# Neighbourhood attention on 192 keys per half block, with three shared transposes per head and products in parts of 128 and 64 keys

## The chip, the cores and the metric

The kernel runs on one core of a Trainium2 chip. The metric is the device time of one execution in microseconds (us), and the number that counts is the median of several. A core has a matmul engine (TensorE, PE in the profile; its weight loads are PEld), a vector engine (VectorE, DVE), an activation engine (ScalarE, ACT), GpSimd (POOL) and SyncE (SP). Here SP issues all the DMAs. Matmuls write into PSUM, which has eight banks of 2 KB in each of its 128 partitions.

## What is computed

A trunk of two layers is applied to two requests of 512 tokens (s = 0 and s = 1), with 1024 channels and 16 heads of 64. Layer 0 is a bidirectional RWKV-7 scan. Layer 1, which is changed here, is attention on a grid of 8 rows by 64 columns: each token attends to all 8 rows and to a window of 16 columns about its own.

```python
GRID_W, WIN_ROWS, WIN_COLS = 64, 8, 16
Q_COL_BLOCK = 16
KEY_COL_SPAN = Q_COL_BLOCK + WIN_COLS          # 32 columns of keys for 16 columns of queries
...
s = jnp.einsum('bnqhd,bsnkhd->bhnqsk', qr, kr)
s = jnp.where(mask, s + bias, NEG_INF)
p = jax.nn.softmax(s.reshape(s.shape[:4] + (-1,)), axis=-1).reshape(s.shape)
return jnp.einsum('bhnqsk,bsnkhd->bnqhd', p, vr)
...
return (o.reshape(bsz, t, D_INNER) * jax.nn.silu(z)) @ w_o + b_o
```

## The kernel before

**Stages.** A prelude projects the first inputs, then a scan phase runs the eight recurrences with projections woven in between. Its instructions stand in an order that a planner in the kernel writes out. Then `rest` (L1724) begins, the part that matters here. There the frame's own scheduler sets the order on every engine: it takes the instructions as the generators emit them, by priority and by a timeline of its own. `rest` makes the remaining in-projections of request 0, the layer-0 output of request 1 (`out0`), the norm after it (`norm0`), the attention output of request 0 (`out1`), the in-projections and the attention of request 1, and `last` (L1502), the output of request 1.

**Matmuls of the projections.** Weights and activations are split into a high and a low part (`halves`, L373: ACT casts the high part, DVE subtracts for the low one). `gemm` (L420) makes a tile of 128x512 outputs with 24 matmuls, L426, L427 and L428 for each of eight slices; they write the tiles `pg` (two banks) or `pm`. L1538 to L1540 are the same for `last`.

**Attention.** `heads(s, p)` (L1394) is a generator that takes one pair of heads. `attention` (L1733) steps it between the slices of the projections, so that its short matmuls stand between the long ones. Tokens are in column order, so that 128 queries are 16 columns: a block n, of which there are four. A pair goes through the blocks in two half steps, `ns` = (0, 1) and (2, 3). There are 16 pairs (8 of each request), so 32 half steps. In each half step stand:

- **scores** (L1421): eight matmuls of 64 queries by 256 keys, on 64x64 tiles of TensorE, one for each block, half block a and head h. They write `sc`, one tile of two banks;
- **softmax**: for each block and head a row of DVE and ACT operations on 256 keys (L1430 adds the bias and takes the maximum, L1432, L1433 is the exponential on ACT, L1434, L1435);
- **transposes** (L1437): two of 128 keys for each block and head, eight in all, into `pt`; ACT copies them to `pts` (L1440);
- **products with v** (L1452): eight matmuls on 128x64 tiles, two key parts of 128 for each block and head, into `po`, one bank that serves the pair through both half steps.

After the second half step L1462 multiplies `po` by the gate z (`tmp` or `oa` takes the result), and for request 1 the result is split at once. Scores and products have a raised priority (`SHP`), and `behind` keeps the products of a half step together.

**Around it.** The bias of a pair comes in two DMAs of 384 KB into one buffer (`NBI` = 1). z is loaded behind the scores of the second half step. q, k, v and z go through DRAM. In `rest` the banks are `pg` 2, `pt` 2, `po` 1, `pm` 1, `sc` 2. `out1` takes `pm` and `pg` in turn, and `last` takes `pg`, `pm`, `pg`, `pt`. Between the two requests stands the norm: `rstds` (L447) sums squares with four matmuls (L452), takes the root on ACT (L455), forms a diagonal on DVE (L460) and spreads it with four matmuls (L464); then L1294 scales eight tiles on DVE, and L1295 adds the residual to them.

Of the kernel before, what the change touches and what calls it, by code (L numbers as in the profile page):

```python
# [10 lines left out]
F32 = mybir.dt.float32  # L11
F32R = mybir.dt.float32r
AF = mybir.ActivationFunctionType
ALU = mybir.AluOpType
# [4 lines left out]
P = 128  # L19
T = 512  # L20
D = 1024
KT = D // P
NP = 8
# [183 lines left out]
        return max([self.t["P"]] + list(self.tiles.values()))  # L207


class Thread:  # L210


# [22 lines left out]
class Trunk:  # L235
# [1 line left out]
    POST0, POST, POST2, POST3, NPA = 0.7, 1.0, 0.15, 0.66, 5  # L237
    HP, HS = (1000, 0), 1000
    SHP = 2000
    OUT1 = ("pm", "pg", "pm", "pg")  # L240
    LOW = 15
    LA = -40
    LATER = (0, 40, 0, 0)
    POST4 = 0.2
    LAST = ("pg", "pm", "pg", "pt")
    PG, PT, NK, NPT = 2, 2, 2, 3
    AHEAD, AHEADW, SCAN_A, SCAN_W = 0, 0, 300, 300
    NAB, NX, NR, NY, NSB, NBI = 2, 2, 2, 2, 4, 1
# [1145 lines left out]
    def heads(self, s, p):  # L1394

        nc = self.nc
        vt, act, gps = nc.vector, nc.scalar, nc.gpsimd
        b = lambda tag, shape=(P, T), n=1, dt=F32: self.t(tag, shape, n, dt, self.ap)
        bias = b("bias", (P, 2, 3, 256), self.NBI)
        for h in range(2):  # L1400
            self.load(bias[:, h].rearrange("p a b -> p (a b)"), self.a["rpb"][2 * p + h])
        q, k, v = (self.load(b(kind, n=2), self.sp[kind, s, p]) for kind in ("q1", "k1", "v1"))
        yield
        vtok = b("vtok", (P, 7, P), self.NK)
        for j0, j1 in ((0, 4), (4, 7)):
            ps = self.p("pt", (P, 4, P))
            for j in range(j0, j1):
                nc.tensor.transpose(ps[:, j - j0], v[:, 64 * j:64 * j + P], self.ident)
            act.copy(vtok[:, j0:j1], ps[:, 0:j1 - j0])
            yield  # L1410
        op = self.p("po", (P, 4, P))
        cols = (0, 8, 24, 32)
        for ns in ((0, 1), (2, 3)):

            sc = self.p("sc", (P, 2, 2, 256))
            with self.tc.high_priority(self.SHP):
                for n in ns:
                    for a in (0, 64):
                        for h in range(2):
                            hs = slice(64 * h, 64 * h + 64)  # L1420
                            nc.tensor.matmul(  # L1421
                                sc[a:a + 64, h, n % 2], q[hs, n * P + a:n * P + a + 64], k[hs, 8 * cols[n]:8 * cols[n] + 256],
                                start=True, stop=True)
            pts = []
            for n in ns:
                pt = self.p("pt", (P, 2, 2, P))
                for h in range(2):
                    sb = b("sb", (P, 256), self.NSB)
                    mx = b("mx", (P, 4), 6)
                    vt.tensor_tensor_reduce(  # L1430
                        sb, sc[:, h, n % 2], bias[:, h, (0, 1, 1, 2)[n]], 1.0, -3.0e38, op0=ALU.add, op1=ALU.max, accum_out=mx[:, 0:1])
                    vt.tensor_scalar(mx[:, 1:2], mx[:, 0:1], -1.0, None, op0=ALU.mult)  # L1432
                    act.activation(sb, sb, AF.Exp, bias=mx[:, 1:2], accum_out=mx[:, 2:3])  # L1433
                    vt.reciprocal(mx[:, 3:4], mx[:, 2:3])  # L1434
                    vt.tensor_scalar(sb, sb, mx[:, 3:4], None, op0=ALU.mult)  # L1435
                    for e in range(2):
                        nc.tensor.transpose(pt[:, h, e], sb[:, e * P:(e + 1) * P], self.ident)  # L1437
                    yield
                pts.append(b("pts", (P, 2, 2, P), self.NPT))
                act.copy(pts[-1], pt)  # L1440
                if n % 2 == 0:
                    yield
            if ns[1] == 3:
                while ("z1", s, p) not in self.sp:
                    yield
                z = self.load(b("z1"), self.sp["z1", s, p])
            last = None
            with self.tc.high_priority(self.SHP):
                for n in reversed(ns):
                    for e in range(2):  # L1450
                        for h in range(2):
                            av = nc.tensor.matmul(  # L1452
                                op[64 * h:64 * h + 64, n], vtok[:, cols[n] // 8 + 2 * e, 64 * h:64 * h + 64], pts[n % 2][:, h, e],
                                start=(e == 0), stop=(e == 1))
                            if n % 2 == 0:
                                self.behind(av, last)
                            else:
                                last = av
            yield
        with self.tc.high_priority(self.HP[s] if p == NP - 1 else 0):  # L1460
            o = self.tmp() if s else self.t("oa", (P, T), NP, F32, self.ap)
            vt.tensor_tensor(o, op.rearrange("p n t -> p (n t)"), z, op=ALU.mult)  # L1462
            if s:
                lo, hi = (self.t("os", (P, T), 2 * NP, F32R, self.ap) for _ in range(2))
                o = self.halves(o, lo, hi)
        self.os[s].append(o)
        yield

    def out1(self, s):
# [32 lines left out]
    def last(self):  # L1502
# [193 lines left out]
    def run(self):  # L1696
        self.todo = [(s, pb) for s in range(2) for pb in range(4)]
        self.made, self.hid, self.shift = set(), {}, {}
        self.did = Counter()
        self.xz, self.os = [], [[], []]  # L1700
        mid, prep, first = ExitStack(), ExitStack(), ExitStack()
        self.banks(mid, pf=1, pm=5 - self.SG - self.ZY, us=1)
        if self.SG:
            self.banks(mid, pg=self.SG)
        self.zs = ExitStack()
        self.banks(self.zs, zy=self.ZY)
        self.gt, self.rt = "zy", "pm"
# [12 lines left out]
        self.AHEAD, self.AHEADW = self.SCAN_A, self.SCAN_W  # L1720
        self.scan_phase(mid)
        self.rest(prep, mid)

    def rest(self, prep, mid):  # L1724
        prep.close()
        mid.close()
        self.banks(self.stack, pg=self.PG, pt=self.PT, po=1, pm=1, sc=1)
        self.rt = "pt"
        self.gt = "pg"
        self.ap = self.pool(self.stack)  # L1730
        queue = [self.heads(0, p) for p in range(self.NPA)]
# [164 lines left out]
```

## Time and profile before

| | before |
|---|---|
| median of 3 runs | 1682.75 us |
| lowest and highest | 1677.2 and 1682.82 us |
| profiled execution, whole time | 1685.84 us |
| its span, first to last instruction | 1684.0 us |
| TensorE busy | 1537.9 us, 91% |
| VectorE busy | 1199.0 us, 71% |
| ScalarE busy | 982.6 us, 58% |
| DMA queue of SP, share of 16 engines | 60.9% |
| mean granted TensorE clock | 0.957 |

A row of the profile names the line, the engine and the operation, then the tile written and the tiles read, the tile shape on TensorE, the shape of the result and how many there were. In a timeline the first two columns are the start and the length in us, and a note in brackets says how long the engine stood idle before and what ended that. Matmuls overlap, so that the time which one takes is the distance between two starts, not its length. An fp32 matmul leaves two records, so that "x16" of L1421 are eight matmuls. The attention starts in this execution at about 1118 us, and all of `rest` lies behind 1085 us.

### The profile page before, as it was taken

How to read it: one execution, taken by the hardware profiler on the slowest of the kernel's cores; microseconds unless marked ns; L12 is line 12 of the kernel's file. 1: busy time of each engine (PE TensorE's matmuls, PEld its weight loads, DVE VectorE, ACT ScalarE, POOL GpSimd, SP SyncE). 2: the span in 40 equal slices, each digit the busy share in tenths (PEclk: the TensorE clock that was granted, in tenths of full speed). 3: DMA queues.
4: the chain of work that ended last, by engine and by line, in shares of the span. 5: the costliest groups of instructions: out<-in, count | busy, mean ns of one | idle time of the engine just before them, and what ended most of it. 6: DMA issues, size and time to landing. Idle time of an engine off the chain costs nothing.

```text
span 1684.0 us, 46244 instructions
## 1 busy us (share of the span) xinstructions
PE 1537.9 (91%) x18880; PEld 1179.6 (70%) x18880; DVE 1199.0 (71%) x2645; ACT 982.6 (58%) x2001; POOL 20.7 (1%) x64
## 2 busy tenths in 40 slices
PE   7989877887989897898899989999999899999997
PEld 6767655665756676676667766778777677777776
DVE  8986788777897887778688996443565666565564
ACT  5444765757767585566756455444566664655562
POOL 0000000000000000000000000000000000000000
PEclk9989887999998999899898999999999999999999
DMA  6435786768675777858774656474565247545563
GB/s 209 163 126 193 242 284 194 229 220 247 216 239 178 221 234 240 242 172 241 222 228 134 219 181 211 139 262 149 185 196 166 95 132 244 189 162 182 168 184 100
DMA packets 237365, 329.98 MB, mean 196 GB/s; under 512 B 53312, under 2 KB 118976, under 8 KB 237152
## 3 DMA queue, kind: packets, MB, share of 16 engines
q1 hardware_dynamic: 237152, 327.01, 60.9%
q8 instruction: 149, 2.44, 0.6%
q14 instruction: 64, 0.52, 0.1%
HBM read 223.52 MB, written 103.42 MB: 194 GB/s over the span
## 4 chain that ended last, share of the span: by engine, by line
PE 52%; DVE 9%; ACT 7%; DMA 5%; issue 3%; SPq 0%; DVEq 0%; ACTq 0%
PE pg L426 6%; PE pg L428 6%; PE pg L427 6%; PE pm L760 5%; PE pm L761 4%; PE pm L762 4%; DMA cab<-dab 2%; PE sc L1421 2%; PE po L1452 2%; PE pf L1077 2%; PE pt L1437 2%; PE zy L1123 1%; PE zy L1154 1%; PE us L1168 1%; ACT X L1163 1%
## 5 line engine op out<-in xcount | busy, mean ns | idle before, releaser
L760 PE MATMUL pm<-act,whi 128*128 128x512 f32 x608 | 271.0, 446 | 21.6 <-ACT act L743 13.7
L761 PE MATMUL pm<-act,whi 128*128 128x512 f32 x608 | 248.0, 408 | 14.2 <-DVE act L745 13.8
L762 PE MATMUL pm<-act,wlo 128*128 128x512 f32 x608 | 246.0, 405 | 0.1
L426 PE MATMUL pg<-act,whi 128*128 128x512 f32 x448 | 182.1, 407 | 2.9 <-DVE tmp L1377 1.9
L427 PE MATMUL pg<-act,whi 128*128 128x512 f32 x448 | 178.1, 398 | 0.0
L428 PE MATMUL pg<-act,wlo 128*128 128x512 f32 x448 | 177.9, 398 | 0.0
L375 ACT CAST whi<-raw 128x512 fp32r<-128x512 f32 x156 | 96.3, 618 | 120.7 <-PE pg L427 61.7
L376 DVE TENSOR_TENSOR wlo<-raw,whi 128x512 fp32r<-128x512 f32 x156 | 107.2, 689 | 82.7 <-ACT whi L375 76.0
L760 PEld LDWEIGHTS pm<-act,whi 128*128 128x128 f32 x608 | 119.0, 196 | 64.1 <-ACT act L743 16.3
L761 PEld LDWEIGHTS pm<-act,whi 128*128 128x128 f32 x608 | 119.7, 197 | 40.6 <-DVE act L745 18.8
L723 DVE TENSOR_TENSOR wlo<-raw,whi 128x512 fp32r<-128x512 f32 x152 | 103.3, 686 | 54.9 <-ACT whi L721 54.7
L762 PEld LDWEIGHTS pm<-act,wlo 128*128 128x128 f32 x608 | 119.0, 196 | 28.0 <-DVE wlo L723 1.6
L721 ACT CAST whi<-raw 128x512 fp32r<-128x512 f32 x152 | 92.6, 619 | 73.3 <-PE pm L761 65.0
L426 PEld LDWEIGHTS pg<-act,whi 128*128 128x128 f32 x448 | 84.8, 189 | 20.9 <-DVE tmp L1377 2.4
L428 PEld LDWEIGHTS pg<-act,wlo 128*128 128x128 f32 x448 | 84.7, 189 | 19.8 <-issue 2.7
L427 PEld LDWEIGHTS pg<-act,whi 128*128 128x128 f32 x448 | 85.0, 190 | 17.1 <-issue 2.3
L967 DVE TENSOR_TENSOR N<-etmp,N 128x30 f32<-128x30 f32 (+14 forms) x240 | 79.8, 332 | 8.3
L1077 PE MATMUL pf<-cab 64*64 64x128 f32 (+1 forms) x2048 | 73.4, 275 | 13.5 <-issue 5.2
L966 DVE TENSOR_TENSOR etmp<-N 128x30 f32<-128x30 f32 (+14 forms) x240 | 78.3, 326 | 3.4
L1163 ACT COPY X<-zy 64x256 f32<-64x256 f32 x128 | 47.0, 367 | 50.3 <-PE zy L1154 41.6
L1077 PEld LDWEIGHTS pf<-cab 64*64 64x64 f32 x2048 | 59.1, 139 | 20.2 <-issue 9.8
L1092 ACT COPY Tm<-pf 128x512 f32<-128x512 f32 x56 | 32.8, 586 | 66.7 <-DVE R L1085 66.2
(432 smaller groups left out, 3319.7 us busy)
## 6 DMA issues: line engine op xcount, KB each, us to landing
dab<-ab SPq DMA_DIRECT2D x32, 1024.0 KB
cab<-dab SPq DMA_DIRECT2D x64, 512.0 KB
raw<-in_w_in_dram SPq DMA_DIRECT2D x128, 256.0 KB
bias<-in_rpb_dram SPq DMA_DIRECT2D x32, 384.0 KB
raw<-in_w_z_dram SPq DMA_DIRECT2D x32, 256.0 KB
dz<-tmp SPq DMA_DIRECT2D x32, 256.0 KB
raw<-in_w_k_dram SPq DMA_DIRECT2D x32, 256.0 KB
dk<-tmp SPq DMA_DIRECT2D x32, 256.0 KB
```

The lines of the kernel that those rows point to most:

```text
L375: self.nc.scalar.copy(hi, src)
L376: (eng or self.nc.vector).tensor_tensor(lo, src, hi.bitcast(F32), op=ALU.subtract)
L426: nc.tensor.matmul(ps, hi, x[k][0], start=(k == 0), stop=False)
L427: nc.tensor.matmul(ps, hi, x[k][1], start=False, stop=False)
L428: nc.tensor.matmul(ps, lo, x[k][0], start=False, stop=(k == KT - 1))
L721: nc.scalar.copy(hi, raw[h])
L723: nc.vector.tensor_tensor(lo, raw.pop(h), hi.bitcast(F32), op=ALU.subtract)
L760: nc.tensor.matmul(ps, hi[:, at], xh, start=(k == 0), stop=False)
L761: nc.tensor.matmul(ps, hi[:, at], xl, start=False, stop=False)
L762: nc.tensor.matmul(ps, lo[:, at], xh, start=False, stop=(k == KT - 1))
L967: vt.tensor_tensor(N[:, q + 1:, :q], tv, N[:, q + 1:, :q], op=ALU.add)
L1077: end = nc.tensor.matmul(f[half(1 - a), h, 0, d, g] if st.last else f[half(1 - a), h, :, d, g], ab[half(h), d, g, 2 * e[d] + a], rt if st. ...
```

## The change

Only the attention and the banks of `rest` change.

- **Keys.** Each half block (64 queries) takes 192 keys of its own, from the start that `FROM` gives in steps of 64, in place of the 256 of its block. Scores, softmax and bias shrink from 256 to 192 keys. The bias of a pair comes in eight DMAs in place of two.
- **Transposes.** The inner loops run over heads first: the probabilities of the two blocks of one head lie side by side (2 x 192 = 3 x 128), and three transposes take them over. A half step has six transposes in place of eight, and `pts` has 384 columns in place of 512.
- **Products.** The 192 keys are a part of 128 (`whole`) and a part of 64, which lies in one half of the partitions: the lower half for the even block, the upper one for the odd block. In two of the four blocks the two half blocks start at different keys, so their products are made for 64 queries at a time. A half step has 12 products, six on 128x64 tiles and six on 64x64 tiles.
- **PSUM.** `sc` becomes two tiles of two banks. The scores take 2 x 192 of 512 columns in each bank, and the products go into the remaining 128 columns of the same tile. `po` and `pm` are gone; `out1` uses `pg` alone, and `last` uses `pg` and `pt`.
- **Gate.** z is loaded as soon as it is there after the first half step, and each half step has its own multiplication of 256 columns (L1485 of the changed kernel) in place of one of 512 (L1462).

```diff
+NKEY, FROM = 192, ((0, 0), (1, 2), (3, 4), (5, 5))
...
-    OUT1 = ("pm", "pg", "pm", "pg")
+    OUT1 = ("pg", "pg", "pg", "pg")
...
-    LAST = ("pg", "pm", "pg", "pt")
+    LAST = ("pg", "pt", "pg", "pt")
...
-        bias = b("bias", (P, 2, 3, 256), self.NBI)
-        for h in range(2):
-            self.load(bias[:, h].rearrange("p a b -> p (a b)"), self.a["rpb"][2 * p + h])
+        bias = b("bias", (P, 2, 3, NKEY), self.NBI)
+        rpb = self.a["rpb"][2 * p:2 * p + 2].rearrange("h p (y j) -> p h y j", y=3)
+        for a, y0, y1, j in ((0, 0, 2, 0), (0, 2, 3, 64), (64, 0, 1, 0), (64, 1, 3, 64)):
+            for h in range(2):
+                self.load(bias[a:a + 64, h, y0:y1], rpb[a:a + 64, h, y0:y1, j:j + NKEY])
...
-            sc = self.p("sc", (P, 2, 2, 256))
+            sc = self.p("sc", (P, 2, T))
...
+                            k0 = 64 * FROM[n][a]
                             nc.tensor.matmul(
-                                sc[a:a + 64, h, n % 2], q[hs, n * P + a:n * P + a + 64], k[hs, 8 * cols[n]:8 * cols[n] + 256],
-                                start=True, stop=True)
+                                sc[64 * a:64 * a + 64, h, NKEY * (n % 2):NKEY * (n % 2) + NKEY], q[hs, n * P + 64 * a:n * P + 64 * a + 64],
+                                k[hs, k0:k0 + NKEY], start=True, stop=True)
...
-                    for e in range(2):
-                        nc.tensor.transpose(pt[:, h, e], sb[:, e * P:(e + 1) * P], self.ident)
+                    if n % 2:
+                        flat = sb.rearrange("p n j -> p (n j)")
+                        for j in range(3):
+                            nc.tensor.transpose(pt[:, j], flat[:, j * P:(j + 1) * P], self.ident)
...
+                for whole in (True, False):
+                    parts = []
+                    for n in ns:
+                        f, odd = FROM[n], n % 2
+                        for a in (slice(0, P),) if f[0] == f[1] else (slice(0, 64), slice(64, P)):
+                            j = f[a.start // 64]
+                            rows = slice(0, P) if whole else slice(64 * odd, 64 * odd + 64)
+                            block = j + odd if whole else j + 2 - 3 * odd
+                            parts.append((n, a, rows, block))
...
+                    for n, a, rows, block in parts:
+                        for h in (1, 0):
                             av = nc.tensor.matmul(
-                                op[64 * h:64 * h + 64, n], vtok[:, cols[n] // 8 + 2 * e, 64 * h:64 * h + 64], pts[n % 2][:, h, e],
-                                start=(e == 0), stop=(e == 1))
+                                sc[64 * h:64 * h + 64, n % 2, 2 * NKEY + a.start:2 * NKEY + a.stop], vtok[rows, block, 64 * h:64 * h + 64],
+                                pts[h][rows, 2 * (n % 2) if whole else 1, a], start=whole and a.start == 0, stop=not whole, skip_group_check=True)
...
+            if ("z1", s, p) in self.sp:
+                if not z:
+                    z.append(self.load(b("z1"), self.sp["z1", s, p]))
+                for sc, at in left:
+                    with self.tc.high_priority(self.HP[s] if p == NP - 1 else 0):
+                        vt.tensor_tensor(
+                            o[:, at].rearrange("p (n t) -> p n t", n=2), sc[:, :, 2 * NKEY:],
+                            z[0][:, at].rearrange("p (n t) -> p n t", n=2), op=ALU.mult)
+                left = []
...
-        self.banks(self.stack, pg=self.PG, pt=self.PT, po=1, pm=1, sc=1)
+        self.banks(self.stack, pg=self.PG, pt=self.PT, sc=2)
```

The scheduler places the instructions anew. Line numbers of the changed kernel are higher by 3 up to the attention, and by 27 behind it. The rows below are of the built programs; the numbers in the names only tell buffers apart.

On TensorE, among the last in-projections of request 0, the kernel before has this where a half step ends (the rows from the products on; the last two matmuls of the projection stand ahead, and transposes of `sb` into `pt` follow):

```order
L427 MATMUL pg_16715<-act_13555,whi_16707 128x512
L428 MATMUL pg_16715<-act_13556,wlo_16708 128x512
L1452 MATMUL po_16556<-pts_16644,vtok_16535 64x128 x4
L1452 MATMUL po_16556<-pts_16591,vtok_16535 64x128 x4
L1421 MATMUL sc_16824<-k_2819_16782,q_2818_16780 64x256 x8
L1437 MATMUL pt_16666<-cc,sb_16667 128x128 x2
L1437 MATMUL pt_16666<-cc,sb_16682 128x128 x2
```

The changed kernel has this on TensorE in the same stage, from the row of the next pair's first score on; one more product of 64x64 and the other seven scores of that pair stand behind it:

```order
L1427 MATMUL sc_16569<-k_2743_16524,q_2742_16522 64x192
L1471 MATMUL sc_16402<-pts_16485,vtok_16271 64x64
L1471 MATMUL sc_16402<-pts_16454,vtok_16271 64x64
L1471 MATMUL sc_16402<-pts_16485,vtok_16271 64x64
L1471 MATMUL sc_16402<-pts_16454,vtok_16271 64x64
L1471 MATMUL sc_16402<-pts_16485,vtok_16271 64x128
L1471 MATMUL sc_16402<-pts_16454,vtok_16271 64x128
L1471 MATMUL sc_16402<-pts_16485,vtok_16271 64x64
L1471 MATMUL sc_16402<-pts_16454,vtok_16271 64x64
L1471 MATMUL sc_16402<-pts_16485,vtok_16271 64x128
L1471 MATMUL sc_16402<-pts_16454,vtok_16271 64x128
L1471 MATMUL sc_16402<-pts_16485,vtok_16271 64x64
```

Products and scores are still neighbours, but a first score often stands ahead of the products now, and the eight scores of one half step are cut into one and seven, or two and six.

On VectorE, at the norm between the two requests, the kernel before has these rows, from the multiplication by the gate of request 0's last pair on (`h` and `hh` are the tiles that the norm scales, `act` is the low part of that last pair):

```order
L1462 TENSOR_TENSOR oa_17993<-po_17818,z_3117_17980 128x512
L1294 SCALAR_TENSOR_TENSOR h_2934_17214<-h_2934_17214,cv,acc_17213 128x512
L1294 SCALAR_TENSOR_TENSOR h_2961_17326<-h_2961_17326,cv,acc_17213 128x512
L1294 SCALAR_TENSOR_TENSOR h_2987_17440<-h_2987_17440,cv,acc_17213 128x512
L1294 SCALAR_TENSOR_TENSOR h_3015_17554<-h_3015_17554,cv,acc_17213 128x512
L1294 SCALAR_TENSOR_TENSOR hh_17668<-hh_17668,cv,acc_17213 128x512
L1294 SCALAR_TENSOR_TENSOR hh_17782<-hh_17782,cv,acc_17213 128x512
L1294 SCALAR_TENSOR_TENSOR hh_17896<-hh_17896,cv,acc_17213 128x512
L1294 SCALAR_TENSOR_TENSOR hh_18001<-hh_18001,cv,acc_17213 128x512
L376 TENSOR_TENSOR act_18034<-oa_17993,act_18035 128x512
```

The changed kernel has these rows at that place on VectorE:

```order
L1485 TENSOR_TENSOR oa_17860<-sc_17861,z_3058_17943 128x256
L460 RECIPROCAL rs_18111<-rs_18111 128x4
L463 TENSOR_SCALAR tmp_18129<-cc,rs_18111 128x128 x4
L1485 TENSOR_TENSOR oa_17860<-sc_17946,z_3058_17943 128x256
L379 TENSOR_TENSOR act_18076<-oa_17860,act_18077 128x512
L1297 SCALAR_TENSOR_TENSOR h_2910_17238<-h_2910_17238,cv,acc_17237 128x512
L1297 SCALAR_TENSOR_TENSOR h_2934_17356<-h_2934_17356,cv,acc_17237 128x512
L1297 SCALAR_TENSOR_TENSOR h_2958_17470<-h_2958_17470,cv,acc_17237 128x512
```

The low part of the last pair has moved from behind the eight scalings of the norm to ahead of them.

More of the change, by code (lines that the diff above doesn't have):

```diff
@@ L1410, in heads @@
             yield
-        op = self.p("po", (P, 4, P))
-        cols = (0, 8, 24, 32)
+        o = self.tmp() if s else self.t("oa", (P, T), NP, F32, self.ap)
+        left, z = [], []
         for ns in ((0, 1), (2, 3)):
-            sc = self.p("sc", (P, 2, 2, 256))
+            sc = self.p("sc", (P, 2, T))
             with self.tc.high_priority(self.SHP):
                 for n in ns:
-                    for a in (0, 64):
+                    for a in range(2):
                         for h in range(2):
@@ L1424, in heads @@
             pts = []
[L1425 to L1428, printed above, removed]
+            for h in range(2):
+                pt = self.p("pt", (P, 3, P))
+                sb = b("sb", (P, 2, NKEY), self.NSB)
+                for n in ns:
+                    x = sb[:, n % 2]
                     mx = b("mx", (P, 4), 6)
                     vt.tensor_tensor_reduce(
-                        sb, sc[:, h, n % 2], bias[:, h, (0, 1, 1, 2)[n]], 1.0, -3.0e38, op0=ALU.add, op1=ALU.max, accum_out=mx[:, 0:1])
+                        x, sc[:, h, NKEY * (n % 2):NKEY * (n % 2) + NKEY], bias[:, h, (0, 1, 1, 2)[n]], 1.0, -3.0e38, op0=ALU.add, op1=ALU.max,
+                        accum_out=mx[:, 0:1])
@@ L1432, in heads @@
                     vt.tensor_scalar(mx[:, 1:2], mx[:, 0:1], -1.0, None, op0=ALU.mult)
-                    act.activation(sb, sb, AF.Exp, bias=mx[:, 1:2], accum_out=mx[:, 2:3])
+                    act.activation(x, x, AF.Exp, bias=mx[:, 1:2], accum_out=mx[:, 2:3])
                     vt.reciprocal(mx[:, 3:4], mx[:, 2:3])
-                    vt.tensor_scalar(sb, sb, mx[:, 3:4], None, op0=ALU.mult)
-                    for e in range(2):
-                        nc.tensor.transpose(pt[:, h, e], sb[:, e * P:(e + 1) * P], self.ident)
+                    vt.tensor_scalar(x, x, mx[:, 3:4], None, op0=ALU.mult)
@@ L1438, in heads @@
+                    if n % 2:
+                        flat = sb.rearrange("p n j -> p (n j)")
+                        for j in range(3):
+                            nc.tensor.transpose(pt[:, j], flat[:, j * P:(j + 1) * P], self.ident)
                     yield
-                pts.append(b("pts", (P, 2, 2, P), self.NPT))
+                pts.append(b("pts", (P, 3, P), self.NPT))
                 act.copy(pts[-1], pt)
-                if n % 2 == 0:
+                if h == 0:
                     yield
@@ L1445, in heads @@
                     yield
-                z = self.load(b("z1"), self.sp["z1", s, p])
-            last = None
+            first = None
             with self.tc.high_priority(self.SHP):
[L1449 to L1452, printed above, removed]
-                                op[64 * h:64 * h + 64, n], vtok[:, cols[n] // 8 + 2 * e, 64 * h:64 * h + 64], pts[n % 2][:, h, e],
-                                start=(e == 0), stop=(e == 1))
[L1455 to L1458, printed above, removed]
@@ L1459, in heads @@
-            yield
+                for whole in (True, False):
+                    parts = []
+                    for n in ns:
+                        f, odd = FROM[n], n % 2
[4 more added lines that the diff above has]
+                            parts.append((n, a, rows, block))
+                    if not whole and len(parts) == 3:
+                        parts = [parts[0], parts[2], parts[1]] if ns[0] else parts
+                    for n, a, rows, block in parts:
+                        for h in (1, 0):
+                            av = nc.tensor.matmul(
+                                sc[64 * h:64 * h + 64, n % 2, 2 * NKEY + a.start:2 * NKEY + a.stop], vtok[rows, block, 64 * h:64 * h + 64],
+                                pts[h][rows, 2 * (n % 2) if whole else 1, a], start=whole and a.start == 0, stop=not whole, skip_group_check=True)
+                            if first is None:
+                                first = av
+                            elif h == 0:
+                                self.behind(av, first)
@@ new lines, in heads @@
+            left.append((sc, slice(ns[0] * P, ns[0] * P + 2 * P)))
+            yield
+            if ("z1", s, p) in self.sp:
[7 more added lines that the diff above has]
+                left = []
@@ L1460, in heads @@
         with self.tc.high_priority(self.HP[s] if p == NP - 1 else 0):
-            o = self.tmp() if s else self.t("oa", (P, T), NP, F32, self.ap)
-            vt.tensor_tensor(o, op.rearrange("p n t -> p (n t)"), z, op=ALU.mult)
             if s:
```

## The prediction

> **What bounds the kernel now.** I read the page's head first, then busy time by stretches, then what TensorE waits for, then its timeline.
>
> ```profile
> span 1684.0 us, 46244 instructions
> PE 1537.9 (91%) x18880; PEld 1179.6 (70%) x18880; DVE 1199.0 (71%) x2645; ACT 982.6 (58%) x2001; POOL 20.7 (1%) x64
> ```
>
> 91% is a mean over stages. In the stretches the columns are: stretch, length, then busy us and count of PE, PEld, DVE, ACT and POOL, granted clock, DMA share, GB/s.
>
> ```profile
> 1085.00:1335.00 250.00, 250.00 (x1522) 198.32 (x1519) 136.33 (x439) 140.90 (x312) 0.00 (x0) 1.00 0.54 179
> 1335.00:1356.00 21.00, 13.35 (x78) 9.64 (x77) 13.99 (x25) 10.28 (x18) 0.00 (x0) 0.76 0.21 67
> 1356.00:1676.00 320.00, 317.28 (x1853) 249.16 (x1851) 186.19 (x534) 169.66 (x365) 0.00 (x0) 1.00 0.54 172
> ```
>
> From 1085 us TensorE is busy without a break, at full clock, but for 21 us about the norm between the requests. VectorE is busy for 136.33 of the first 250 us, ScalarE for 140.90. So in the attention each instruction that TensorE no longer runs shortens the kernel by its pitch, and work taken from the other engines is worth nothing. TensorE's longest waits behind 1110 us (sum, count, longest):
>
> ```profile
> PE pm L427 <- DVE act L376: 4.8, 1, 4.8
> PE pg L426 <- DVE tmp L1377: 1.9, 1, 1.9
> PE pm L426 <- ACT act L375: 1.2, 1, 1.2
> PE pg L426 <- ACT whi L375: 1.0, 2, 0.8
> ```
>
> No row names a DMA, `po`, `pts` or `sb` as late: the transfers and the softmax chain are in time. Three of the rows lie in the 21 us.
>
> **The pitches.** One end of a half step, start, length, then the row:
>
> ```profile
> 1182.17 0.39 PE L427 MATMUL pg<-act,whi 128*128 128x512 f32 x1
> 1182.40 0.39 PE L428 MATMUL pg<-act,wlo 128*128 128x512 f32 x1
> 1182.72 1.10 PE L1452 MATMUL po<-pts,vtok 128*64 128x128 f32 x16
> 1183.74 1.09 PE L1421 MATMUL sc<-k,q 64*64 64x256 f32 x16
> 1184.77 1.10 PE L1437 MATMUL pt<-cc,sb 128*128 128x128 f32 x8
> 1185.62 0.48 PE L426 MATMUL pg<-act,whi 128*128 128x512 f32 x1
> 1185.93 0.40 PE L427 MATMUL pg<-act,whi 128*128 128x512 f32 x1
> ```
>
> From start to start a long matmul takes 0.227 us, eight products 1.02, eight scores 1.03, eight transposes 0.85 (0.107 each). Elsewhere one score stands alone:
>
> ```profile
> 1233.60 0.64 PE L1421 MATMUL sc<-k,q 64*64 64x256 f32 x2
> 1234.17 1.09 PE L1452 MATMUL po<-pts,vtok 128*64 128x128 f32 x16
> 1235.19 1.09 PE L1421 MATMUL sc<-k,q 64*64 64x256 f32 x14
> 1236.21 0.50 PE L426 MATMUL pg<-act,whi 128*128 128x512 f32 x1
> 1236.55 0.39 PE L427 MATMUL pg<-act,whi 128*128 128x512 f32 x1
> ```
>
> One score takes 0.57 us until the next kind begins, eight (or seven, the third row) 1.02. A score uses one of four corners of the array, so eight are two rounds. A round of 256 keys is therefore 0.44 us, and a hand-over to another tile shape 0.14. Likewise the products are 0.88 + 0.14, 0.11 each. Entering from the long matmuls costs 0.09 more than their pitch (1182.40 to 1182.72), going back 0.08 to 0.11 (1185.62 to 1185.93, 1236.21 to 1236.55). With the hand-over, one entry and exit cost about 0.34 together.
>
> No row shows the new shapes, but the end of the scan has neighbours of them:
>
> ```profile
> 1043.03 0.69 PE L1168 MATMUL us<-X,Tm 128*64 128x64 f32 x16
> 1043.55 0.64 PE L1172 MATMUL zy<-X,R 128*64 128x64 f32 x16
> 1045.01 1.10 PE L1077 MATMUL pf<-cab 64*64 64x128 f32 x32
> 1045.93 0.64 PE L1123 MATMUL zy<-S,cab 64*64 64x64 f32 x32
> 1046.39 0.41 PE L1129 MATMUL zy<-V,AK 64*64 64x64 f32 x16
> ```
>
> Eight matmuls of 64 columns on 128x64 tiles take 0.52 us (0.06 each). On 64x64 tiles with all corners in use sixteen of 128 columns take 0.92 (0.0575 each), sixteen of 64 columns 0.46 (0.029).
>
> **The change, part by part: TensorE**, for each of 32 half steps.
>
> - Scores: two rounds of 192 keys in place of 256; 0.44 x 192 / 256 = 0.33, so 2 x 0.11 = 0.22 us less, 7.0 in all. The rate per column is taken as unchanged, as it is between the rows of 128 and 64 columns.
> - Transposes: two fewer, 2 x 0.107 = 0.21, or 6.8 in all.
> - Products: before 8 x 0.11 = 0.88. After, `whole` has two of 128 columns and four of 64: 2 x 0.11 + 4 x 0.06 = 0.46. The part of 64 keys has two of 128 and four of 64 columns. The even block uses the lower rows and the odd one the upper, each for 128 columns a head, so four corners are loaded alike: 2 x 0.0575 + 4 x 0.029 = 0.23, if the row halves run side by side. If they do not, it is 0.46, since half the array stands still. I take 0.23, as the nearest rows have that shape. That is 0.19 less, or 6.1 in all; by the other end it is 7.4 us less gain.
>
> Together 19.9 us. The new order gives some of it back. In the TensorE rows of the built program, 11 half steps have their scores cut so that they need three rounds (one and seven six times, two and six five times), 11 x 0.33 = 3.6 us; before, three were, 3 x 0.44 = 1.3. That is 2.3 lost. Hand-overs between the short shapes rise from 23 to 44, since the products now have two shapes, 21 x 0.14 = 2.9, and entries from the long matmuls from 44 to 48, 4 x 0.34 = 1.4. So 19.9 - 2.3 - 4.3 = 13.3 us. A hand-over could cost nothing where the corners left by one shape are already free for the next; then up to 4.3 more is gained.
>
> **The norm between the requests.** The place in the timeline (brackets: idle before, and what ended it), then two stretches:
>
> ```profile
> 1342.13 0.62 ACT L375 CAST act<-oa 128x512 fp32r<-128x512 f32 x1
> 1342.27 2.74 DVE L1294 SCALAR_TENSOR_TENSOR h<-h,cv,acc 128x512 f32<-128x512 f32 x4 [0.74 <-ACT acc L466]
> 1342.80 0.50 PE L426 MATMUL pm<-act,whi 128*128 128x512 f32 x1 [1.19 <-ACT act L375]
> 1344.92 2.73 DVE L1294 SCALAR_TENSOR_TENSOR hh<-hh,cv,acc 128x512 f32<-128x512 f32 x4
> 1347.57 0.68 DVE L376 TENSOR_TENSOR act<-oa,act 128x512 fp32r<-128x512 f32 x1
> 1348.31 0.80 PE L427 MATMUL pm<-act,whi 128*128 128x512 f32 x1 [4.78 <-DVE act L376]
> 1351.21 0.79 PE L426 MATMUL pg<-act,whi 128*128 128x512 f32 x1 [0.83 <-ACT whi L375]
> 1342.00:1345.00 3.00, 0.73 (x2) 0.30 (x2) 2.73 (x5) 0.75 (x2) 0.00 (x0) 1.00 0.00 0
> 1345.00:1355.00 10.00, 5.86 (x13) 3.99 (x14) 8.96 (x16) 6.11 (x12) 0.00 (x0) 0.50 0.21 61
> ```
>
> The first slice of `out1` needs the low part of the last pair. VectorE makes it at 1347.57, behind eight scalings of 0.68 us. TensorE waits 4.78 us for it, and then the granted clock is 0.50 until about 1355. In 12.2 us (1342.80 to 1355) it runs 2 + 13 = 15 matmuls that need 15 x 0.227 = 3.4, so 8.8 us are lost. In the changed order the low part stands ahead of the scalings. It still needs the gate and the cast, which I leave at about 1 us of waiting. `out1` then has only the two banks of `pg` and no third, about 1 us more, and 0.5 for the cast of `whi` behind. I take 2.4 us as left, and 6.4 gained. The bounds are 8.8, all of it, and about 2.4, if the clock halves all the same.
>
> The Trainium skill, "TensorE: Matmul & The Clock Gate", Part 1: The HAM clock gate, says that the clock falls to half after an idle window of about 3.4 us and comes back after a busy one. The trace agrees that a wait of 4.78 us was followed by 0.50. By that rule waits of about 1 us each keep the full clock and the gain is 6.4; without it, the gain is the lower bound, 2.4.
>
> **Costs I put at nothing.** VectorE and ScalarE work on 192 keys in place of 256, have half as many copies of `pts`, and get a second gate multiplication; TensorE at 250.00 of 250.00 us hides all of it. `out1` on `pg` alone and `last` without `pm` cost nothing outside the norm if a bank is emptied within one slice, 24 x 0.227 = 5.4 us, which the copy of 0.7 us does.
>
> **The sum.** 13.3 + 6.4 = 19.7 us. Against the profiled execution 1685.84 - 19.7 = 1666.1. It stands 3.1 above the median of the three runs, so the median should become 1663.0 us.
>
> **Rivals.**
>
> ```profile
> 1200.01 0.81 SPq L331 DMA_DIRECT2D bias<-in_rpb_dram  x2
> SPq L331 <- DVE wlo L376: 121.6, 65, 7.8
> DVE tmp L1462 <- PE po L1452: 12.1, 7, 6.6
> ```
>
> *Smaller gain*: the row halves of the products take turns (7.4 us), or the clock halves at the norm all the same (4.0), or both: 1667 to 1674.4.
>
> *More gain*: hand-overs and cuts cost nothing (4.3 + 2.3) and the norm loses nothing (2.4): down to 1654.
>
> *No gain, the bias on SP*: two issues took 0.81 us, so eight take 3.2, which is 2.4 more for a pair and 38 in all. SP also issues the weights, and behind them stand the splits and TensorE. For it speaks that one queue carries everything. Against it, SP stood waiting for VectorE for 121.6 us in 65 places, up to 7.8, so it is ahead of its readers, and no TensorE row waits for a transfer. If half of it came through: 1663 + 19 = 1682; all of it: 1701, of which I believe little.
>
> *Slower, the scores wait for the gate*: the products now lie in the `sc` tile, which is free for the scores two half steps later only when VectorE has multiplied by z (L1485). Before, `po` was free of the scores. By the pitches above, the shortest distance on TensorE from a half step's products to the scores that reuse its tile is 3.6 us of work in request 0, about 6.5 in request 1. It decides from there: if the multiplication, or z, comes about 4.5 us behind the products, 0.9 us is lost in each half step, 32 x 0.9 = 29, and the time is 1692. For it: VectorE runs in order, with softmax rows ahead of the multiplication. Against it: VectorE itself stood idle for `po` in seven places, 12.1 us, so it comes to the multiplication early, and it is a little over half busy.
>
> That the change does not do what it says is excluded: the built rows have 192 keys, six transposes and products of both shapes.
>
> **How the numbers follow.** The likeliest case, 1658 to 1670 about 1663, has 0.66; smaller gain 0.16; more gain 0.04; the bias 0.08; the gate 0.06. The range goes from 1655 (the bound of more gain) to 1675 (both parts of smaller gain) and leaves out the last two cases and the tails, under 0.2. A measurement here can tell 0.5%, 8.4 us, from no change. Faster than 1674.3: 0.66 + 0.13 + 0.04 = 0.83. Within the bound: 0.10 (0.03 of smaller gain, 0.06 of the bias, 0.01 of the gate). Slower: 0.07 (0.02 and 0.05).
>
> **What would show it.** Right: from a block's first score to the next kind 0.80 us for eight scores (0.33 x 2 + 0.14), 0.64 for six transposes; a 64x64 part of about 0.23 us plus a hand-over; in the stretch of the norm a clock near 1.00 and no wait above 2 us. Wrong: a 64x64 part of 0.46, a clock of 0.50 behind the norm, or TensorE rows in which `sc` waits for VectorE at L1485, or long matmuls wait for `wlo` or a DMA. If the attention's stretch shrinks by far less than 13 us with all pitches as said, the cuts and hand-overs are mis-sized.

## The result and the profile after

The changed kernel took 1669.38 us (median of 4 runs, 1666.08 to 1671.44) against 1682.78 for the kernel before, a ratio of 0.9926 (95% interval 0.9901 to 0.9951). Measured again beside the experiments it had a ratio of 0.996 (0.9942 to 0.9979). The two intervals overlap. The scan, which the change does not touch, took between 1068.9 and 1077.5 us in the profiled executions of this study, and that moves the whole times. So the runs are compared below by their stretch behind the scan, from the start of the last matmul into `zy` to the last matmul's end (its start and the pitch of 0.23 us). It was 590.3 us before, and 580.6 and 579.9 in two executions of the changed kernel: about 10 us less, or 0.6%. The page of the changed kernel begins:

```profile
span 1669.6 us, 46734 instructions
PE 1523.9 (91%) x19072; PEld 1168.3 (70%) x19072; DVE 1183.1 (71%) x2661; ACT 968.5 (58%) x2001; POOL 20.6 (1%) x64
```

I cut the stretch at three places that both kernels have: the first matmul of the norm (L452, L455 after), the end of the 56th long matmul behind it, and the 225th long matmul from the end. In the kernel before (the columns are those of the prediction's stretches):

```profile
1084.95:1337.79 252.84, 252.60 (x1550) 200.16 (x1546) 136.33 (x439) 141.54 (x314) 0.00 (x0) 1.00 0.54 178
1337.79:1365.03 27.24, 19.64 (x88) 14.85 (x89) 21.39 (x37) 14.30 (x26) 0.00 (x0) 0.81 0.31 97
1365.03:1616.56 251.53, 249.61 (x1519) 195.84 (x1517) 147.94 (x446) 140.82 (x301) 0.00 (x0) 1.00 0.57 184
1616.56:1675.23 58.67, 58.66 (x298) 46.32 (x296) 30.29 (x77) 23.45 (x55) 0.00 (x0) 1.00 0.38 117
```

In the changed kernel:

```profile
1081.44:1329.52 248.08, 247.55 (x1637) 194.66 (x1632) 128.24 (x447) 134.70 (x313) 0.00 (x0) 1.00 0.55 174
1329.52:1347.98 18.46, 16.45 (x98) 13.04 (x97) 15.60 (x30) 13.15 (x23) 0.00 (x0) 1.00 0.27 87
1347.98:1593.64 245.66, 242.79 (x1564) 193.04 (x1562) 144.74 (x453) 135.04 (x301) 0.00 (x0) 0.99 0.58 184
1593.64:1662.03 68.39, 62.51 (x349) 48.10 (x347) 34.27 (x90) 25.33 (x61) 0.00 (x0) 0.98 0.41 127
```

The attention of request 0 became 4.8 us shorter, the norm 8.8, the middle of request 1 5.9. The last stretch became 9.7 us longer, and TensorE, which never stood still there before, is idle for 5.9 us of it. Its last boundary shifts a little work: behind it stand three blocks of products and two of scores in place of two and one. The run e3 below shifts it in the same way with the old widths, and there the middle is 249.4 us, 2.2 shorter than before, and the last stretch 61.2, 2.5 longer. So some 2 of the 5.9 us are moved work, and about 7 of the 9.7 are lost. Where a kernel moves that boundary, the two last stretches are taken together ("behind the norm": 310.2 before, 314.0 after).

**The norm.** Timeline of the changed kernel (start, length):

```profile
1333.97 0.69 DVE L379 TENSOR_TENSOR act<-oa,act 128x512 fp32r<-128x512 f32 x1 [0.68 <-ACT act L378]
1333.99 0.73 PE L429 MATMUL pg<-act,whi 128*128 128x512 f32 x2 [0.35 <-ACT act L378]
1334.58 2.73 DVE L1297 SCALAR_TENSOR_TENSOR h<-h,cv,acc 128x512 f32<-128x512 f32 x4
1334.72 0.50 PE L430 MATMUL pg<-act,whi 128*128 128x512 f32 x1
1336.52 0.50 PE L429 MATMUL pg<-act,whi 128*128 128x512 f32 x1 [0.60 <-ACT os L1504]
```

The low part (L379) stands ahead of the scalings (L1297). The wait of 4.78 us is gone. What is left are 0.35 us for the cast, 0.60 for a bank, and 1.06 for the diagonal (L463; it was 0.62 for L460 before), and the clock in the stretch is 1.00 in place of 0.81.

**The blocks.** A block with its scores cut in two and six, one of products alone, and the end of a block of products:

```profile
1484.01 0.39 PE L429 MATMUL pg<-act,whi 128*128 128x512 f32 x1
1484.33 0.54 PE L1427 MATMUL sc<-k,q 64*64 64x192 f32 x4
1484.80 1.05 PE L1471 MATMUL sc<-pts,vtok 128*64 128x64 f32 x24
1485.69 0.81 PE L1427 MATMUL sc<-k,q 64*64 64x192 f32 x12
1486.43 0.50 PE L430 MATMUL pg<-act,whi 128*128 128x512 f32 x1
```

```profile
1595.54 1.05 PE L1471 MATMUL sc<-pts,vtok 128*64 128x64 f32 x24
1596.53 0.50 PE L431 MATMUL pg<-act,wlo 128*128 128x512 f32 x1
```

```profile
1328.75 0.46 PE L1471 MATMUL sc<-pts,vtok 64*64 64x128 f32 x12
1329.14 0.55 PE L1447 MATMUL pt<-cc,sb 128*128 128x128 f32 x3
```

A block of products takes 0.99 us (1595.54 to 1596.53). Its six products on 64x64 tiles take 0.39 until another shape follows (1328.75 to 1329.14), which is 0.23 and a hand-over; so the row halves run side by side. Where scores follow, which have the same shape, the next begins 0.89 us behind the first product (1484.80 to 1485.69), 0.1 less than 0.99: of the second hand-over little is left there.

**The end.** What TensorE waited for behind 1590 us (sum, count, longest), where before it waited for nothing:

```profile
PE sc L1427 <- DVE tmp L1485: 2.4, 1, 2.4
PE pt L1447 <- ACT pts L1450: 1.4, 1, 1.4
PE pt L1447 <- DVE sb L1443: 1.3, 2, 1.1
PE pt L1413 <- DMA v<-dv: 0.7, 1, 0.7
```

The timeline there, of SP, VectorE and TensorE:

```profile
1603.79 0.34 SPq L331 DMA_DIRECT2D dz<-tmp  x1
1607.50 0.34 SPq L334 DMA_DIRECT2D z<-dz  x1
1610.23 0.76 DVE L1485 TENSOR_TENSOR tmp<-sc,z 128x256 f32<-128x256 f32 x2 [0.49 <-DMA z<-dz]
1610.71 1.53 PE L1427 MATMUL sc<-k,q 64*64 64x192 f32 x32 [2.41 <-DVE tmp L1485]
```

```profile
1618.02 0.40 PE L1567 MATMUL pg<-act,os 128*128 128x512 f32 x1
1619.49 0.97 PE L1447 MATMUL pt<-cc,sb 128*128 128x128 f32 x4 [1.07 <-DVE sb L1443]
1622.48 0.55 PE L1447 MATMUL pt<-cc,sb 128*128 128x128 f32 x3 [1.40 <-ACT pts L1450]
```

The pair before last of request 1 (p = 6) finished its products at 1596.5 us. Its z is projected second to last, is stored at 1603.79 and reloaded at 1607.50, and the gate runs at 1610.23. Until then it holds both `sc` tiles. So the last pair's sixteen scores come together at 1610.71, and its softmax is still running when the long matmuls beside it are used up at 1618.02.

### The profile page after: what moved, and what is told of

Its sections match the earlier page's. It is cut to its first block, busy times and chain, and to the rows that moved or that the text cites. A ratio compares the mean times of both kernels' runs of the same rounds, so it can differ in the third digit from the quotient of the medians.

```text
span 1669.6 us, 46734 instructions
## 1 busy us (share of the span) xinstructions
PE 1523.9 (91%) x19072; PEld 1168.3 (70%) x19072; DVE 1183.1 (71%) x2661; ACT 968.5 (58%) x2001; POOL 20.6 (1%) x64
## 4 chain that ended last, share of the span: by engine, by line
PE 48%; DVE 10%; ACT 9%; DMA 5%; issue 3%; SPq 1%; DVEq 0%; ACTq 0%
PE pg L430 6%; PE pg L429 6%; PE pg L431 6%; PE pm L763 5%; PE pm L764 4%; PE pm L765 4%; DMA cab<-dab 2%; PE sc L1471 2%; PE pf L1080 2%; PE sc L1427 1%; PE pt L1447 1%; PE zy L1157 1%; PE us L1171 1%; DVE ab L844 1%; PE zy L1126 1%
## 5 line engine op out<-in xcount | busy, mean ns | idle before, releaser
L429 PE MATMUL pg<-act,whi 128*128 128x512 f32 x480 | 192.9, 403 | 2.8 <-DVE tmp L1380 1.9
L430 PE MATMUL pg<-act,whi 128*128 128x512 f32 x480 | 191.4, 399 | 0.0
L431 PE MATMUL pg<-act,wlo 128*128 128x512 f32 x480 | 190.8, 398 | 0.0
L379 DVE TENSOR_TENSOR wlo<-raw,whi 128x512 fp32r<-128x512 f32 x156 | 107.0, 688 | 86.1 <-ACT whi L378 81.2
L429 PEld LDWEIGHTS pg<-act,whi 128*128 128x128 f32 x480 | 90.6, 189 | 21.5 <-DVE tmp L1380 2.1
L430 PEld LDWEIGHTS pg<-act,whi 128*128 128x128 f32 x480 | 90.8, 189 | 19.4 <-issue 2.0
L431 PEld LDWEIGHTS pg<-act,wlo 128*128 128x128 f32 x480 | 90.7, 189 | 19.5 <-issue 1.7
L1441 ACT ACTIVATE sb<-sb,mx 128x192 f32<-128x192 f32 x128 | 57.1, 449 | 24.7 <-DVE mx L1440 24.5
```

The source lines that it names most:

```text
L379: (eng or self.nc.vector).tensor_tensor(lo, src, hi.bitcast(F32), op=ALU.subtract)
L429: nc.tensor.matmul(ps, hi, x[k][0], start=(k == 0), stop=False)
L430: nc.tensor.matmul(ps, hi, x[k][1], start=False, stop=False)
L431: nc.tensor.matmul(ps, lo, x[k][0], start=False, stop=(k == KT - 1))
```

## The experiments

All times are in us, from one profiled execution of each; "all" is the stretch behind the scan, and the ratio is that of the whole time to the kernel before, with its 95% interval.

| run | request 0 | norm | behind the norm | all | ratio |
|---|---|---|---|---|---|
| before | 252.8 | 27.2 | 310.2 | 590.3 | 1 |
| changed | 248.1 | 18.5 | 314.0 | 580.6 | 0.9926 (0.9901 to 0.9951) |
| changed, again | 248.2 | 18.5 | 313.2 | 579.9 | 0.996 (0.9942 to 0.9979) |
| e1, products copied out | 249.1 | 18.5 | 314.5 | 582.1 | 0.9932 (0.9905 to 0.9959) |
| e2, scores uncut | 246.7 | 18.5 | 314.3 | 579.4 | 0.9934 (0.9909 to 0.9959) |
| e3, before with low part first | 252.9 | 18.6 | 310.6 | 582.0 | 0.9979 (0.9957 to 1.0) |
| e4, z earlier | 248.1 | 18.5 | 308.9 | 575.5 | 0.9909 (0.9879 to 0.9938) |
| e5, before without `pm` | 253.4 | 27.9 | 312.0 | 593.3 | 0.9995 (0.9961 to 1.003) |
| e6, z earlier, scores uncut | 246.9 | 19.3 | 309.3 | 575.5 | 0.9886 (0.9846 to 0.9926) |
| e7, bias in two loads of other rows | 247.6 | 18.1 | 312.4 | 578.1 | 0.9908 (0.9878 to 0.9938) |
| e8, bias in two loads | 247.6 | 18.5 | 312.8 | 578.8 | 0.9904 (0.9875 to 0.9933) |
| e9, e4 and e8 | 247.6 | 18.1 | 308.1 | 573.7 | 0.9883 (0.9848 to 0.9918) |
| e10, e8 with z in the middle | 247.6 | 18.1 | 313.4 | 579.1 | 0.9896 (0.9844 to 0.9949) |

**The changed kernel again.**

> The changed kernel once more, beside the others on one chip. Between the two profiled executions the stretch behind the scan shrank by 9.65 us (571.08 to 561.43 from the last instruction of the scan on TensorE), and the scan itself, which the change does not touch, by 3.6. If the 3.6 are chance, this run has a ratio to the kernel before of 0.9943 (-9.65 us); if they belong to the change, of 0.992 (-13.3).

0.9943 was expected for one case, 0.992 for the other; 0.996 is nearer to the first, and its interval holds the first alone. The 3.6 us of the scan are taken as chance, since this run's scan was 1.4 us longer than that of before. The two executions agree within 0.8 us behind the scan, and a difference there of less than about 1 us decides nothing.

**e3: the norm by itself**, in the kernel before (`low` is the low part of the last pair):

```diff
+                self.low = self.nc.vector.tensor_tensor(hi, src, lo.bitcast(F32), op=ALU.subtract)
...
-            nc.vector.scalar_tensor_tensor(h, h, self.vec("post0", k), rstd, op0=ALU.mult, op1=ALU.mult)
+            one = nc.vector.scalar_tensor_tensor(h, h, self.vec("post0", k), rstd, op0=ALU.mult, op1=ALU.mult)
+            self.behind(one, self.low)
```

> The kernel before, but the eight scalings of the norm are ordered behind the low part of request 0's last pair. Theory: the 8.8 us that the changed kernel gained in the norm come from this order alone: about 7 to 8.8 us less than before, 1675, with a clock near 1.00 in the stretch of the norm. Rival: they come from the gate in two halves and the banks of `out1`, which stay as before here: at most 2 us less, 1681.

```profile
1336.08:1354.40 18.32, 16.50 (x87) 12.98 (x88) 14.98 (x28) 12.49 (x22) 0.00 (x0) 1.00 0.21 62
```

The norm fell from 27.2 to 18.6 us (the line ends at the start of the 56th long matmul, 0.24 us ahead of the cut of the table), all of what the changed kernel gained there, with a clock of 1.00. Request 0 and the part behind the norm are within 0.4 us of before. So in the stretch of the norm the order alone does it. The whole time does not show it: the median was 1679.76 us, nearer to the rival's 1681 than to 1675, and the ratio of 0.9979 is worth 3.5 us, where the stretch behind the scan fell by 8.3.

**e1: the gate no longer holds the tile.**

```diff
+            at = slice(ns[0] * P, ns[0] * P + 2 * P)
+            if s and p == 6:
+                act.copy(o[:, at].rearrange("p (n t) -> p n t", n=2), sc[:, :, 2 * NKEY:])
+                left.append((o[:, at].rearrange("p (n t) -> p n t", n=2), at))
+            else:
+                left.append((sc[:, :, 2 * NKEY:], at))
...
```

> The changed kernel, but ScalarE copies the products of the pair before last of request 1 (p = 6) out of `sc`, so that the multiplication by z no longer holds the tile. Theory: the gate of that pair, whose z is made second to last, holds both `sc` tiles; the last pair's scores come late, all sixteen at once, and its softmax has too little work beside it. Without it the 2.4 us wait on the gate, the waits for `sb` and `pts` and the half clock behind them go: the last 225 long matmuls and what stands among them take about 60 us in place of 68.4, and the time is about 1661 (8 to 9 us less than the changed kernel). Rival: it is the third bank that is missing behind the projections (no `pm` for the second slice of `last`); then only the 2.4 us go, about 1667.

Neither case came. The 2.4 us wait went and nothing was won. SP, ScalarE and TensorE in this run:

```profile
1606.40 0.34 SPq L331 DMA_DIRECT2D dz<-tmp  x1
1614.46 0.34 SPq L331 DMA_DIRECT2D dz<-tmp  x1
1615.06 1.57 SPq L334 DMA_DIRECT2D raw<-in_w_ao_dram  x2
1619.27 0.62 ACT L378 CAST whi<-raw 128x512 fp32r<-128x512 f32 x1 [3.11 <-DMA raw<-in_w_ao_dram]
1620.60 0.85 ACT L1450 COPY pts<-pt 128x384 f32<-128x384 f32 x2
1621.13 0.79 PE L1570 MATMUL pt<-h,os 128*128 128x512 f32 x1 [3.69 <-ACT pts L1450]
```

The scores came early now, but a copy of `pts` stood on ScalarE behind casts of the weights of `last`, whose loads stood on SP behind a store of z (`dz`). That store, at 1614.46, is the last pair's; the one of p = 6 stands at 1606.40. So the wait had moved to something else, and these rows do not show that the z of p = 6 is the cause of both, as the next expectation has it.

**e4: z of that pair earlier.**

```diff
-        for p, cs in [(p, range(4)) for p in range(6)] + [(6, range(3)), (7, range(3)), (6, (3,)), (7, (3,))]:
+        for p, cs in [(p, range(4)) for p in range(6)] + [(6, range(3)), (6, (3,)), (7, range(3)), (7, (3,))]:
```

> The changed kernel, but the projection of z for the pair before last of request 1 (p = 6) stands ahead of q, k and v of the last pair, in place of behind them. In the run with the copy the 2.4 us wait went, but another of 3.7 us took its place: the copy of `pts` stood on ScalarE behind casts of `last`'s weights, whose loads stood on SP behind the store of z. Theory: the late z is at the root of both, so that here the last 225 long matmuls and what is among them take about 60 us in place of 68.3 and all behind the scan about 572 in place of 580. Rival: what is missing is work beside the last softmax, since `last` has one bank less in front; then waits for `sb` or `pts` stay and the tail takes 65 us or more.

```profile
PE pt L1413 <- DMA v<-dv: 1.5, 1, 1.5
PE sc L1427 <- DMA k<-dk: 1.4, 1, 1.4
```

5.1 us less behind the norm, the last stretch 62.75 in place of 68.39. Against the second execution of the changed kernel it is 4.3. The waits for the gate, for `pts` and for `sb` are gone there; for the last pair's k and v there are now 1.4 and 1.5 us, as one slice less of projections stands between them and the scores. Some 3 us more were expected. So the late z is the larger part of the loss, not all.

**e5: the bank**, in the kernel before.

```diff
-    OUT1 = ("pm", "pg", "pm", "pg")
+    OUT1 = ("pg", "pg", "pg", "pg")
...
-    LAST = ("pg", "pm", "pg", "pt")
+    LAST = ("pg", "pt", "pg", "pt")
```

> The kernel before, with the banks of `out1` and `last` as in the changed kernel (`pg` alone; `pg` and `pt` in turn), `pm` left unused. Theory (late z holds `sc`): the tail of 225 long matmuls stays at 58.7 us, within 1; the norm stays near 27, since the low part still comes last. Rival (the bank is missing): the tail grows by 4 us or more.

3.0 us more in all: 1.8 behind the norm (2.1 in the last stretch) and 0.6 each in request 0 and in the norm. Neither case: the bank costs something, but less than the rival asked. The norm stayed near 27, so without the other order the banks gain nothing there.

**e2 and e6: the cut scores.**

```diff
-                            nc.tensor.matmul(
+                            one = nc.tensor.matmul(
...
+                            if ns[0] == 0 and self.did["av"]:
+                                self.behind(one, self.av)
...
+            self.av, self.did["av"] = av, 1
```

e6 leaves the last pair of request 0 out of this and has the early z of e4.

> The changed kernel, but the scores of a pair's first half step are ordered behind the products of the pair before, so that none stands ahead of them. Theory: cut scores cost a third round of 0.33 us and a second change of shape of 0.14 in some 13 half steps, since products and scores in one piece took 1.72 us and with two or four records of scores ahead 2.19: 13 x 0.4 = 5 us less, about 1664. Rival: a first score fills a place where TensorE would wait, so that nothing is won: 1669, and rows in which the products wait appear.

> The changed kernel with z of p = 6 early, and with the scores of a first half step behind the products of the pair before, except at the last pair of request 0. In the run where all were ordered so, a block of cut scores and products fell from 2.49 to 2.03 us and from 2.19 to 1.73, twelve times, 5.5 us in all, but the last pair of request 0 came 3.3 us later to the norm, and nearly nothing was left. Theory: with that pair spared the 5 us remain; beside the tail's 8 that is about 567 behind the scan, 1657 in all. Rival: the other waits of that run (plain long matmuls 1.9 us more, a block of transposes 1.2) come with the order itself: 571 behind the scan.

A block of e2:

```profile
1489.56 0.39 PE L429 MATMUL pg<-act,whi 128*128 128x512 f32 x1
1489.87 1.05 PE L1473 MATMUL sc<-pts,vtok 128*64 128x64 f32 x24
1490.76 0.82 PE L1427 MATMUL sc<-k,q 64*64 64x192 f32 x16
1491.51 0.50 PE L430 MATMUL pg<-act,whi 128*128 128x512 f32 x1
```

From the long matmul ahead to the one behind it is 1.95 us, against 2.42 for the cut block (1484.01 to 1486.43): 0.47 less, as a round of 0.33 and a hand-over of 0.14 make. But 0.5 to 1.2 us is all that was left in e2, and nothing in e6. The order moved other things: in e2 TensorE waited 3.0 us for v in three places (in the changed kernel 0.7 in one), and 1.02 for the softmax of request 0's last pair, just ahead of the norm. The price of a cut was right. That the cut hid a wait is what these rows suggest; no run takes it by itself.

**e7 and e8: the bias.** Both load it in two DMAs. e7 takes the first 192 columns of every row, so that some rows have the bias of other keys; e8 has the table laid out by half block ahead of the kernel. The edit is that of e8, without the layout:

```diff
-        rpb = self.a["rpb"][2 * p:2 * p + 2].rearrange("h p (y j) -> p h y j", y=3)
-        for a, y0, y1, j in ((0, 0, 2, 0), (0, 2, 3, 64), (64, 0, 1, 0), (64, 1, 3, 64)):
-            for h in range(2):
-                self.load(bias[a:a + 64, h, y0:y1], rpb[a:a + 64, h, y0:y1, j:j + NKEY])
+        for h in range(2):
+            self.load(bias[:, h].rearrange("p a b -> p (a b)"), self.a["rpb"][2 * p + h])
...
```

> The changed kernel with the bias of a pair in two DMAs in place of eight; all rows take the first 192 columns, so for some rows it is the bias of other keys. Theory: SP has time for the six more issues; behind the scan 580 us, within 1. Rival (issues on SP delay the weights): 2 us less or more.

> The changed kernel with the bias laid out in memory by the 192 keys of each half block, so that a pair's bias is right and comes in two DMAs (384 and 192 keys are the same table in another order; nothing is computed for it). The run with two DMAs and the wrong rows took 578.1 us behind the scan, against 580.6 and 579.9. If the six issues on SP cost something, this one gives 577 to 578.5 too; if that difference was chance of the order, 579.5 or more.

In the changed kernel SP issues the pieces like this:

```profile
1194.90 1.76 SPq L334 DMA_DIRECT2D bias<-in_rpb_dram  x3
```

That is 0.59 us apiece, not the 0.4 of the prediction; eight come to some 4.7 for a pair, against 0.81 for two, 62 us for sixteen pairs. Of these 1.4 us (e8) to 2.2 (e7) came through, about the limit of what two executions can tell.

**e9 and e10: together.**

> The changed kernel with both: z of p = 6 early (575.5 us behind the scan) and the bias in two DMAs of its own layout (2 us less, if it is not chance). If the two add up, 573 to 574 behind the scan, and 1662 in all by the difference of 17 to the kernel before; if the bias only mattered in the tail, where z is now out of the way, 575.5.

> As the run with both, but z of p = 6 stands between k and v of the last pair, so that there is a slice more of long matmuls between the last pair's first loads and its scores. Where z stood ahead of q, k and v, TensorE still waited 1.5 us for v and 1.4 for k. Theory: with z in the middle the wait for k goes and that for v stays (it is loaded last), 572 to 574 behind the scan. Rival: the gate of p = 6 comes a slice or two later and holds `sc` again, 576 to 578.

e9 has 573.7 us behind the scan, 16.6 less than before and 6 to 7 less than the changed kernel; it has the shortest stretch and the lowest ratio of the study, 0.9883, with 1664.99 us (e6 had 1664.57, beside a kernel before of 1686.91 in place of 1684.19). In e10 neither case came. 579.1 is longer than both; the gate held `sc` for only 0.84 us, but v, whose projection now stands behind that z, came late.

```profile
1615.02 1.75 PE L1411 MATMUL pt<-cc,v 128*128 128x128 f32 x7 [5.06 <-DMA v<-dv]
```

## Why the prediction was right, and where not

The direction and the range held; the forecast gain of 19.7 us did not. About 10 came, as the stretch behind the scan shows. That the range held is in part luck. The scan happened to be 3.6 us shorter in the first profiled execution, and the second median of the changed kernel, 1677.94 (beside 1684.05 for the kernel before), lies above the 1675 of the range. The upper part of the range stood for row halves that take turns and a clock that halves at the norm, and neither came.

- **TensorE bounds the attention: right.** Shorter short blocks shortened the first and third stretch while VectorE and ScalarE stayed half idle.
- **The pitches: right.** `whole` with its hand-over took 0.60 us in nearly every half step (0.46 + 0.14), the part of 64 keys 0.39 (0.23 + 0.14), eight scores among long matmuls added 0.90 us in place of 1.12, and eight took 0.75 to 0.81 us to the next kind (0.80 forecast). The rival of taking turns (0.46) is excluded. A full hand-over from the 64x64 products to scores was counted, and 0.28 us in place of 0.39 was measured.
- **The sum for the attention: too large.** 13.3 us were forecast. Request 0 gave 4.8 of its half, 6.65. In request 1 the middle gave 5.9, of which some 2 is work moved behind the boundary. So 8 to 9 came through ahead of the last stretch. Part of the difference is the bias (1.4 to 2.2, costed at nothing). In request 0 the short blocks also stand in 54 places in place of 40, and each return to long matmuls costs 0.1; but in the middle of request 1 they stand in 50 in place of 68. There TensorE waited 0.99 us for ScalarE (L1525; 1.94 in the second execution), which it did not before, and in the first execution the clock was 0.50 for 3.4 us from 1394.8 on, a loss of 1.7. What else is missing in request 0 stays open.
- **The norm: right in mechanism, too small.** 8.8 us in place of 6.4, and e3 shows that the order alone gives it. I left 1 us for the gate and the cast, which cost 0.35, 1 for a bank that cost 0.60, and 0.5 for the cast of `whi`, for which no wait is left.
- **The step that failed** is "`out1` on `pg` alone and `last` without `pm` cost nothing outside the norm", with the rival of the gate priced only for all half steps alike. (That price does not fit its own distances either: at 4.5 us the 6.5 of request 1 lose nothing, so it is 16 x 0.9.) The rival's mechanism was there, at one place, and with it a sign that the prediction had named: `sc` waited for L1485. It was the gate of the pair before last, which waits for z, not for VectorE, and holds `sc` from 1596.5 to 1610.2. Behind the norm 6.65 us less were forecast and 3.8 more came. About 7 of these 10 were lost in the last stretch (68.4 against 61.2 in e3). e4 gives 4.3 to 5.1 of them back, and e5 puts the bank at about 2 behind the norm in the kernel before. e9 still waits 1.5 us for k and 1.6 for v of the last pair, and no run sorts these from the rest.
- **What would have shown it:** the order of the built program has at its end sixteen scores in one piece, 24 long matmuls, and nine transposes in one piece, where the kernel before has its transposes in groups of four, four and eight with other work between. I looked for the rival by the shortest distance on TensorE, and not for the time at which z is made.

## What to carry to other kernels

Where an engine is saturated, count its pitches: they came out nearly as forecast here, and the sum in request 0 to two thirds (4.8 of 6.65 us). Then look where it is not saturated, at the ends, since a buffer that now serves two purposes is held there until the latest of its readers' inputs arrives. A wait that is removed at such an end can uncover the next one (2.4 us for the gate became 3.7 for a copy): look for one change that ends several waits, here the place of z. An order that looks wasteful, like cut scores, may be what hides a transfer.

## What the runs showed of the hardware

The clock fell in the last stretch of the changed kernel though no wait within 12 us ahead of it was above 1.40 us. Stretches of one us (length, busy us and count of PE, clock, DMA share, GB/s):

```profile
1618.00:1619.00 1.00, 0.42 (x2) 1.00 0.19 72
1619.00:1620.00 1.00, 0.46 (x2) 1.00 0.36 59
1621.00:1622.00 1.00, 0.08 (x1) 1.00 0.00 0
1623.00:1624.00 1.00, 1.00 (x25) 0.73 0.03 8
1624.00:1625.00 1.00, 1.00 (x14) 0.50 0.00 0
1626.00:1627.00 1.00, 1.00 (x4) 0.57 0.00 0
```

TensorE was busy for 2.30 us of the five from 1618 on (with 0.82 and 0.52 in the two that are not shown, 1620 and 1622), for the most part with transposes, and in the sixth the clock fell. In the norm, waits of 1.06, 0.35 and 0.60 us with work between them left it at 1.00, and so did the wait of 2.41 us at 1610.71. So the prediction's reading by the single wait is too coarse.

Two more figures of the traces bear on it. By the shares 0.73 and 0.57 the clock was 0.50 from 1623.46 to 1626.86, for 3.4 us, and it was 0.50 for 3.4 us from 1394.8 on too; in the kernel before it was so for 10.2 us from 1345.0 on, three times as long. And one wait had both outcomes: 1.87 us for L1380 was followed by 0.50 in the first execution of the changed kernel (1395 to 1398), and by 1.00 in the second (at 1398.98). The busy share does not decide alone either. In the 3.41 us up to the fall at 1623.45 TensorE was busy for 1.83, but in the second execution 1.56 in the 3.41 us from 1418.88 on left the clock at 1.00. The Trainium skill, "TensorE: Matmul & The Clock Gate", Part 1: The HAM clock gate, speaks of activity in a window of about 3.4 us. The lengths of 3.4 and 10.2 us agree with such a window; how little work in it lowers the clock, the runs do not show.
